# Gates and values by seven products of half the width: a gated MLP's up projection after Strassen, residual stream in DRAM

## The chip, the core and the metric

The kernel runs on one core of a Trainium2 chip. The time is the device time of one execution in microseconds (us). The core has a matrix engine (TensorE, PE in the profile, its weight loads PEld), a vector engine (VectorE, DVE), a scalar engine (ScalarE, ACT), GpSimd (POOL), and SyncE (SP), whose queue issues most of the DMA transfers. PE reads its operands from the on-chip memory SBUF and adds its products into PSUM, which holds eight banks of 128 partitions x 512 floats; ACT and DVE read both memories.

## What is computed

One layer of a diffusion backbone over 512 latent tokens and 256 context tokens of width 2048, in float32: modulation vectors from `c`, two attention mixers (eight heads of differential attention, eight of latent attention), an output projection, and a gated MLP. The change is in the MLP, which is this, with `h` of 512 x 2048, `w_up` of 2048 x 11264, `w_down` of 5632 x 2048:

```
h2 = modulate(rmsnorm(x, norm2_w), sh2, s2)
g, u = split(h2 @ w_up)                               # 512 x 5632 each
g = conv over tokens of width 3 (centred) + bias
x = x + g2 * ((silu(g) * u) @ w_down)
return rmsnorm(x, final_w)
```

## The kernel before

Everything lies feature-first: a tile has 128 features on the partitions and the tokens along the row, so an activation tile is 128 x 512. A matrix product in float32 is made of three passes over operands in a faster 32-bit format: each operand is split into a high part (a rounding cast on ACT, line 75) and a low part (the difference, on DVE, line 76), and `mm3` (lines 96 to 101) adds high x high, high x low and low x high into the same PSUM tile, one `matmul` each.

Weights come from DRAM in blocks of 128 x 1024 (512 KB) through `wblock` (lines 82 to 89): a DMA on SP's queue into `wr`, then the split into `wh` and `wl`; each of the three has three buffers. Eight weight tiles of 128 x 128 are in one block.

PSUM: two `s` tiles of 1024 columns (two banks each, `s_tile`) and four `b` tiles of one bank (`b_tile`).

The stages are: the modulation vectors and first projection (to about 180 us), the input projection (to about 470), the two attentions (to about 880), the output projection (to about 1050), the second norm, and the MLP (from about 1062 to 2511), then the final norm and the stores.

The MLP has 44 pairs. A pair `ft` is 128 features of the gate and the 128 features of the value that multiply them. `up(ft)` (lines 736 to 745) makes both, the gate into the left half of an `s` tile and the value into the right half: for each, 16 row blocks of K (2048 / 128) times three matmuls of 128 x 512. `first_pair` makes the first two pairs together, row block by row block, in both `s` tiles, since their operands `hx` come from the norm just then. `activate` (lines 747 to 760) is the convolution (ACT, then two fused multiplies on DVE), SiLU on ACT, the product on DVE and the split into `ah` and `al`. After four pairs (a chunk; `FC` is 4, and there are eleven) `down` (lines 762 to 774) multiplies the four activations by their part of `w_down`: 16 output tiles, each four row blocks of three matmuls into a `b` tile, and a fused multiply and add on DVE (line 771) into `x1`, the residual stream, which stays in SBUF in the 16 tiles of the pool `bp`. The chunks overlap: the four pairs of chunk c are issued before `down` of chunk c - 1. The last `down` runs in two halves of 256 tokens, so that the final norm of the first half lies beside the second.

Pools are reused tile by tile: an instruction that writes a buffer waits for the last reader of the tile that was there. The language's scheduler puts the instructions of each engine in a fixed order when the program is built, by the order of the code and its own estimate of when each can start, and inserts the semaphore waits. On the chip each engine goes through its list in that order.

Of the kernel before, what the change touches and what calls it, by code (L numbers as in the profile page):

```python
# [17 lines left out]
P = 128  # L18
D = 2048
KT = D // P  # L20
T = 512
# [13 lines left out]
FC = 4  # L35
NFC = NFT // FC
# [13 lines left out]
def layer_kernel(ctx: ExitStack, tc: tile.TileContext, small, rope, c_row, cc_row, x_t, ctx_t, ada, ada_k,  # L50
                 w_g0, w_f, w_v, w_uqn, w_uqr, w_ukv, w_o, w_up0, w_up, w_dn, out_t):
    nc = tc.nc
# [49 lines left out]


    sm = ctx.enter_context(tc.tile_pool(name="sm", bufs=1))
    sm.tile([P, 96], F32, name="edge")
    rim = ctx.enter_context(tc.tile_pool(name="rim", bufs=1, side="right"))
    rim.tile([P, 120], F32, name="rim")


    smt = cst.tile([P, NSMALL], F32, name="smt")  # L110
# [3 lines left out]
        o = OFF[name] + j  # L114
        return smt[:, o:o + 1]

    ropet = cst.tile([P, 2, T], F32, name="ropet")
# [52 lines left out]
    def a2k(dt=F32):  # L170
        return ap_.tile([P, 512], dt, tag="a2k", name=nm("a2k"))
# [246 lines left out]
    q = rtmp()  # L418
# [176 lines left out]
    mb = None  # L595
    nxt = latent_pair(0)
    da.release()
    bp = ctx.enter_context(tc.tile_pool(name="bp", bufs=16, reuse_waits="tile"))

    def b2k(dt=F32):  # L600
        return bp.tile([P, 512], dt, tag="b2k", name=nm("b2k"))
# [38 lines left out]
    mb.release()  # L640
    ma.release()
    mc.release()
    ps_b.release()
    ps_b = ctx.enter_context(tc.tile_pool(name="ps_c", bufs=4, space=PSUM, reuse_waits="tile"))


    ap_ = tc.alloc_tile_pool(name="ap2", bufs=32, side="right", reuse_waits="tile")
    wo = tc.alloc_tile_pool(name="wo", bufs=1, reuse_waits="tile")
    cb = wo.tile([P, D], F32, name="cb2")
# [16 lines left out]
    def token_norm(pool, ss, last):  # L666

        n = ss.shape[1]
        po = b_tile()[:, :n]
        pe.matmul(po, ones32, ss, start=True, stop=False)  # L670
        for i, x in enumerate(last):
            q = pool.tile([P, T], F32, tag="sq", name=nm("sq"), bufs=2)[:, :n]
            sc.square(q, x)
            pe.matmul(po, ones32, q, start=False, stop=i == len(last) - 1)
        r, t1, t2 = (pool.tile([P, T], F32, tag=g, name=nm(g), bufs=1)[:, :n] for g in ("nr", "n1", "n2"))
        rstd(r, po, D, t1, t2)
        return r

# [29 lines left out]
    r = token_norm(wo, ss, x1[12:])  # L708
    hx = []
    for dt in range(KT):  # L710
        t = wo.tile([P, T], F32, tag="xr", name=nm("xn"), bufs=3)
        ve.tensor_tensor(t, x1[dt], r, op=ALU.mult)
        h = wo.tile([P, T], F32, tag="h", name=nm("h"), bufs=2)
        sc.activation(h, t, AF.Identity, scale=a2[:, dt:dt + 1], bias=modx[:, 48 + dt:49 + dt])
        hl = a2k(F32R), a2k(F32R)
        split(hl[0], hl[1], h)
        hx.append(hl)
    wo.release()


    ff = tc.alloc_tile_pool(name="ff", bufs=1, reuse_waits="tile")

    def first_pair():

        ss_ = [s_tile(), s_tile()]
        for kb in range(8):
            wh, wl = wblock(w_up0[kb])
            for j in range(2):
                kt = kb * 2 + j
                for i in range(4):  # L730
                    o = j * 512 + i * P
                    mm3(ss_[i // 2][:, (i % 2) * 512:(i % 2 + 1) * 512], (wh[:, o:o + P], wl[:, o:o + P]), hx[kt],
                        kt == 0, kt == KT - 1)
        return [activate(ft, s) for ft, s in enumerate(ss_)]

    def up(ft):
        s = s_tile()
        for i in range(2):
            o = s[:, i * 512:(i + 1) * 512]
            for hf in range(2):  # L740
                wh, wl = wblock(w_up[ft - 2, i, hf])
                for j in range(8):
                    kt = hf * 8 + j
                    mm3(o, (wh[:, j * P:(j + 1) * P], wl[:, j * P:(j + 1) * P]), hx[kt], kt == 0, kt == KT - 1)
        return activate(ft, s)

    def activate(ft, s):
        g, u = s[:, :512], s[:, 512:]
        t = ff.tile([P, T], F32, tag="t", name=nm("t"), bufs=2)
        sc.activation(t, g, AF.Identity, scale=col("cw", NFT + ft), bias=col("cb", ft))  # L750
# [5 lines left out]
        a = ff.tile([P, T], F32, tag="sq", name=nm("a"), bufs=2)  # L756
        ve.tensor_tensor(a, t, u, op=ALU.mult)
        hl = [ff.tile([P, T], F32R, tag=g_, name=nm(g_), bufs=6) for g_ in ("ah", "al")]
        split(hl[0], hl[1], a)
        return hl  # L760

    def down(c, acts, ts=slice(0, T), then=None):
        for dp in range(8):
            wh, wl = wblock(w_dn[c, dp])
            for i in range(2):
                dt = dp * 2 + i
                po = b_tile()[:, :ts.stop - ts.start]
                for f in range(FC):
                    o = f * 256 + i * P
                    mm3(po, (wh[:, o:o + P], wl[:, o:o + P]), [a[:, ts] for a in acts[f]], f == 0, f == FC - 1)  # L770
                ve.scalar_tensor_tensor(out=x1[dt][:, ts], in0=po, scalar=modx[:, 80 + dt:81 + dt],  # L771
                                        in1=x1[dt][:, ts], op0=ALU.mult, op1=ALU.add)
                if then:
                    then(dt)

    acts = first_pair() + [up(ft) for ft in range(2, FC)]
    for c in range(1, NFC):
        nxt = [up(c * FC + f) for f in range(FC)]
        down(c - 1, acts)
        acts = nxt  # L780


    norms = []
    for th in range(2):
        ts = slice(th * 256, (th + 1) * 256)
        ss = ff.tile([P, 256], F32, tag="ss", name=nm("ss"), bufs=2)
        down(NFC - 1, acts, ts, lambda dt: add_square(ff, ss, x1[dt][:, ts], dt == 0) if dt < 12 else None)
        norms.append(ss)
    exp_ln_tables()
    for th in range(2):  # L790
        ts = slice(th * 256, (th + 1) * 256)
        r = token_norm(ff, norms[th], [x[:, ts] for x in x1[12:]])
        for dt in range(KT):
            y = a2k()[:, :256]
            ve.scalar_tensor_tensor(out=y, in0=x1[dt][:, ts], scalar=col("fw", dt), in1=r, op0=ALU.mult, op1=ALU.mult)
            nc.sync.dma_start(out_t[dt][:, ts], y)
    ff.release()
    ap_.release()


# [77 lines left out]
```

## Time and profile before

| | us |
|---|---|
| median of 3 runs (lowest to highest) | 2538.99 (2534.21 to 2539.63) |
| the profiled execution | 2537.23 |
| its span, first to last instruction | 2535.5 |
| PE busy | 2457.9 |
| DVE busy | 1368.1 |
| ACT busy | 820.6 |
| POOL busy | 97.7 |
| DMA, HBM read and written | 331.68 MB and 23.34 MB, 140 GB/s |

The profile is one execution. Its page gives the busy time of each engine, the same in 40 slices with the clock granted to PE (PEclk, 1.00 is full) and the DMA share, the chain of waits that ended last, and groups of instructions by line: busy time, mean duration in ns, idle time of the engine just before them and what released it. The views asked of the trace beside it are the timeline (start, duration, engine, line, tiles), the same groups by shape, and the sums over stretches of time (windows). A name such as `wh` stands for all buffers of that name. Matmuls are pipelined: a duration runs from the start to the landing of the result and overlaps the next ones, so the distance of starts is what one costs.

### The profile page before, as it was taken

Reading aid. Unit: us, or ns where it says so; the run is one execution under the profiler, and the core shown is the slowest. Engines: PE = TensorE matmul, PEld = TensorE weight load, DVE = VectorE, ACT = ScalarE, POOL = GpSimd, SP = SyncE. Lnnn points to the kernel's source line nnn. Section 1 sums busy time; section 2 is a strip of 40 time slices with the busy share of each in tenths; the row PEclk is TensorE's granted clock in tenths of the full one; section 3 lists DMA queues with packets and bytes.
Section 4 is the critical chain, followed back from the end, with each engine's and each line's share of the span. In section 5 each row is a group of like instructions: output and inputs, shape, how many; then the busy total and the mean of one; then the engine's idle time right before and its main releaser. Section 6 shows DMA issues by size and latency. Waiting matters only on the chain.

```text
span 2535.5 us, 29404 instructions
## 1 busy us (share of the span) xinstructions
PE 2457.9 (97%) x11852; PEld 2003.8 (79%) x11852; DVE 1368.1 (54%) x1779; ACT 820.6 (32%) x1189; POOL 97.7 (4%) x90
## 2 busy tenths in 40 slices
PE   7999999999899999899999999999999999999996
PEld 3778887777777788778888888888888888888886
DVE  4778876498787875533444434343434343434356
ACT  4342221265555622432222222222222222222223
POOL 0000000221100012000000000000000000000003
PEclk9999999999999999999999999999999999999998
DMA  7868898544211185223323223323323333233234
GB/s 276 286 220 320 325 333 307 173 136 135 89 58 55 49 314 197 84 85 99 100 92 100 100 92 100 99 93 100 98 93 100 95 96 100 94 98 100 93 102 146
DMA packets 105214, 356.94 MB, mean 141 GB/s; under 512 B 11379, under 2 KB 22131, under 8 KB 96627
## 3 DMA queue, kind: packets, MB, share of 16 engines
q1 hardware_dynamic: 104118, 351.92, 41.7%
q0 software_dynamic: 960, 3.15, 0.3%
q8 instruction: 93, 1.52, 0.2%
q14 instruction: 43, 0.35, 0.0%
HBM read 331.68 MB, written 23.34 MB: 140 GB/s over the span
## 4 chain that ended last, share of the span: by engine, by line
PE 90%; DVE 6%; ACT 2%; POOL 1%; issue 1%; DMA 1%; DVEq 0%; ACTq 0%; POOLq 0%
PE s L99 16%; PE s L100 16%; PE s L101 16%; PE b L100 10%; PE b L99 10%; PE b L101 10%; PE s L475 3%; PE f L99 1%; PE pt L487 1%; PE f L100 1%; DVE m L477 1%; PE f L101 1%; DVE p L533 1%; PE b L212 1%; PE po L99 1%; POOL p L532 1%
## 5 line engine op out<-in xcount | busy, mean ns | idle before, releaser
L76 DVE TENSOR_TENSOR wl<-wr,wh 128x1024 fp32r<-128x1024 f32 (+2 forms) x382 | 458.8, 1201 | 724.8 <-ACT wh L75 712.9
L75 ACT CAST wh<-wr 128x1024 fp32r<-128x1024 f32 (+2 forms) x382 | 394.3, 1032 | 1142.2 <-PE s L100 668.7
L99 PE MATMUL s<-a2k,wh 128*128 128x512 f32 x1600 | 625.9, 392 | 15.2 <-ACT a2k L75 6.4
L100 PE MATMUL s<-a2k,wh 128*128 128x512 f32 x1600 | 625.9, 391 | 0.0
L101 PE MATMUL s<-a2k,wl 128*128 128x512 f32 x1600 | 625.6, 391 | 0.0
L99 PEld LDWEIGHTS s<-a2k,wh 128*128 128x128 f32 x1600 | 301.4, 189 | 79.2 <-ACT a2k L75 7.6
L100 PEld LDWEIGHTS s<-a2k,wh 128*128 128x128 f32 x1600 | 301.6, 189 | 62.2 <-issue 1.2
L101 PEld LDWEIGHTS s<-a2k,wl 128*128 128x128 f32 x1600 | 301.5, 188 | 62.3 <-issue 0.6
L100 PE MATMUL b<-al,wh 128*128 128x512 f32 (+1 forms) x768 | 285.2, 371 | 0.0
L101 PE MATMUL b<-ah,wl 128*128 128x512 f32 (+1 forms) x768 | 285.2, 371 | 0.0
L99 PE MATMUL b<-ah,wh 128*128 128x512 f32 (+1 forms) x768 | 285.2, 371 | 0.0
L771 DVE SCALAR_TENSOR_TENSOR b2k<-b,modx,b2k 128x512 f32<-128x512 f32 (+1 forms) x192 | 135.1, 705 | 169.0 <-PE b L101 168.7
L164 DVE CUSTOM_DVE_ANT_0 ada<-ada,cb,smt 128x2048 f32<-128x2048 f32 x64 | 151.4, 2368 | 45.6 <-DMA ada<-in_ada 45.4
L100 PEld LDWEIGHTS b<-al,wh 128*128 128x128 f32 x768 | 144.7, 188 | 25.0
L101 PEld LDWEIGHTS b<-ah,wl 128*128 128x128 f32 x768 | 144.7, 188 | 24.9
L99 PEld LDWEIGHTS b<-ah,wh 128*128 128x128 f32 x768 | 144.7, 188 | 24.9
L99 PE MATMUL b<-a2k,wh 128*128 128x512 f32 x304 | 119.7, 394 | 1.6 <-ACT wh L75 1.6
L100 PE MATMUL b<-a2k,wh 128*128 128x512 f32 x304 | 119.5, 393 | 0.0
L101 PE MATMUL b<-a2k,wl 128*128 128x512 f32 x304 | 118.5, 390 | 0.0
L664 POOL TENSOR_TENSOR ss<-ss,sq 128x256 f32<-128x256 f32 (+1 forms) x33 | 45.2, 1371 | 1764.0 <-ACT sq L663 1762.9
L477 DVE TENSOR_REDUCE m<-s 128x1 f32<-128x768 f32 x96 | 90.5, 950 | 15.6 <-PE s L475 15.3
L76 DVE TENSOR_TENSOR wtl<-pt,wth 128x512 fp32r<-128x512 f32 x92 | 63.2, 687 | 20.8 <-ACT wth L75 20.1
(250 smaller groups left out, 2963.7 us busy)
## 6 DMA issues: line engine op xcount, KB each, us to landing
wr<-in_w_up SPq DMA_DIRECT2D x176, 512.0 KB, 3.4
ada<-in_ada SPq DMA_DIRECT2D x64, 1024.0 KB, 6.0
wr<-in_w_dn SPq DMA_DIRECT2D x96, 512.0 KB, 3.4
wr<-in_w_f SPq DMA_DIRECT2D x34, 512.0 KB, 6.4
adak<-in_ada_k SPq DMA_DIRECT2D x32, 512.0 KB, 6.7
ada<-in_ada SPq DMA_DIRECT2D x32, 512.0 KB, 6.8
wr<-in_w_o SPq DMA_DIRECT2D x32, 512.0 KB, 3.5
wr<-in_w_v SPq DMA_DIRECT2D x16, 512.0 KB, 6.8
```

The costliest lines, as they stand in the source:

```text
L75: sc.copy(dst_h, src)
L76: ve.tensor_tensor(dst_l, src, dst_h.bitcast(F32), op=ALU.subtract)
L99: pe.matmul(out, st[0], mv[0], start=start, stop=False, **kw)
L100: pe.matmul(out, st[0], mv[1], start=False, stop=False, **kw)
L101: pe.matmul(out, st[1], mv[0], start=False, stop=stop, **kw)
L164: ve.tensor_tensor_reduce(out=junk, in0=w, in1=vec, op0=ALU.mult, op1=ALU.add, scale=1.0, scalar=col("b_ada", j), accum_out=dst[:, j:j + 1])
L212: pe.matmul(acc[32 * c:32 * c + 32, :n], cpad[:, kt], src(kt), start=j == 0, stop=j == 3)
L475: pe.matmul(s[:, c0:c1], a, b[:, c0:c1], start=i == 0, stop=i == len(mms) - 1)
L477: ve.tensor_reduce(out=m, in_=s[:, :TT], axis=AX.X, op=ALU.max, negate=True)
L487: pe.transpose(pt[:, qt * P:(qt + 1) * P], ws[qt][:, kt * P:(kt + 1) * P], ident)
L664: gp.tensor_tensor(out=ss, in0=ss, in1=q, op=ALU.add)
L771: ve.scalar_tensor_tensor(out=x1[dt][:, ts], in0=po, scalar=modx[:, 80 + dt:81 + dt], in1=x1[dt][:, ts], op0=ALU.mult, op1=ALU.add)
```

## The change

For pairs 4 to 43 the products for gate and value are regrouped. K is cut in two halves (row blocks 0 to 7 and 8 to 15), the tokens in two halves of 256, and the two outputs of a pair (gate and value) are the third cut. That is a 2 x 2 by 2 x 2 block product, and Strassen's scheme (in Winograd's form) makes it with seven block products in place of eight, each of 8 row blocks x 128 columns x 256 tokens, and additions of operands and results:

- The operand sums `t1` to `t4` over halves of h (with low parts, like all operands) are made once, after the second norm (`sums`), and kept in SBUF; `h11` (first half of K, first half of the tokens) and `h2` (second half of K, all tokens) are kept too. `h12` is needed for the first four pairs only.
- The weight sums are made for every pair on DVE (four sums of 128 x 1024 in `strassen`), and each of the seven weight blocks is then split into high and low.
- Results gather in `y` and `z` (256 columns in each half of an `s` tile) and `x` (a `b` tile); `m1`, `m5` and `u2` are copied to SBUF by ACT on the way, and DVE adds them to the others.

Pairs 0 to 3 are made the former way; as the first half of K now lies in two tiles by tokens, its matmuls there are 256 wide (`classical`). `first_pair` uses the four `b` tiles, and takes the row blocks in another order (0, 4, 1, 5, ...). The norm's shift and scale go into one fused multiply and the split itself.

The residual stream goes to DRAM: `x1_d` is written after the output projection (DMA on POOL's queue), `down` loads each tile before it adds to it (DMA on SP's queue, three buffers `xs`), and stores it again (POOL's queue). The last `down` loads into 16 tiles and keeps them there. The order of the chunks is now: first pair of chunk c, `down` of chunk c - 1, the other three pairs. `ah` and `al` have five buffers (six before).

The diff, cut to its core:

```diff
+    x1_d = [dram.tile([P, T], F32, name=f"x1_d{i}") for i in range(KT)]
...
             x1.append(x)
+            gp.dma_start(x1_d[dt], x)
...
+    def normed(kt):
+        b = modx[:, 48 + kt:49 + kt]
+        h = hf[kt] = hp.tile([P, T], F32, tag="h", name=nm("h"), bufs=5)
+        ve.scalar_tensor_tensor(out=h, in0=x1[kt], scalar=a2[:, kt:kt + 1], in1=r, op0=ALU.mult, op1=ALU.mult)
...
+        for (hh, hl), c in parts:
+            sc.activation(hh, h[:, c], AF.Identity, bias=b)
+            ve.scalar_tensor_tensor(out=hl, in0=h[:, c], scalar=b, in1=hh.bitcast(F32), op0=ALU.add, op1=ALU.subtract)
...
+    def sums(j):
+        a, c, b = hf[j], hf[j + 8], modx[:, 56 + j:57 + j]
...
+        ve.tensor_tensor(d1, a[:, h1], a[:, h0], op=ALU.subtract)
+        ve.scalar_tensor_tensor(out=d2, in0=c[:, h1], scalar=b, in1=d1, op0=ALU.add, op1=ALU.subtract)
+        put_away(t1, d1)
+        ve.scalar_tensor_tensor(out=d1, in0=c[:, h1], scalar=db[:, j:j + 1], in1=a[:, h1], op0=ALU.add, op1=ALU.subtract)
+        put_away(t3, d1)
+        ve.scalar_tensor_tensor(out=d1, in0=c[:, h0], scalar=b, in1=d2, op0=ALU.add, op1=ALU.subtract)
+        put_away(t2, d2)
+        put_away(t4, d1)
+
+    def classical(out, kt, w, start, stop):
+        if kt < 8:
+            mm3(out[:, h0], w, h11[kt], start, False, True)
+            mm3(out[:, h1], w, h12[kt], False, False, True)
+        else:
+            mm3(out, w, h2[kt], False, stop, True)
...
+    def strassen(ft):
+        s = s_tile()
+        y, z, x = s[:, :HT], s[:, 512:512 + HT], b_tile()[:, :HT]
...
+        def product(out, w, hs, start, stop=True):
+            wh, wl = (wp.tile([P, 1024], F32R, tag=g, name=nm(g), bufs=3) for g in ("wh", "wl"))
+            split(wh, wl, w)
+            for j in range(8):
+                mm3(out, (wh[:, j * P:(j + 1) * P], wl[:, j * P:(j + 1) * P]), hs[j], start and j == 0, j == 7, True)
+
+        def kept(src, tag):
+            t = mm.tile([P, HT], F32, tag=tag, name=nm(tag), bufs=1)
+            sc.copy(t, src)
+            return t
+
+        a11, a21, a22, a12 = raw(0, 0, wp), raw(1, 0, wp), raw(1, 1, mm), raw(0, 1, mm)
...
+        product(y, a11, h11, True)                                  # P1
+        m1 = kept(y, "m1")
+        w = mm.tile([P, 1024], F32, tag="ws", name=nm("ws"), bufs=1)
+        ve.tensor_tensor(w, a21, a22, op=ALU.add)
+        product(z, w, t1, True)                                     # P2
+        m5 = kept(z, "m5")
+        ve.tensor_tensor(w, w, a11, op=ALU.subtract)
+        product(y, w, t2, False)                                    # P3
+        u2 = kept(y, "u2")
+        product(x, a12, h21, True)                                  # P4
+        ve.tensor_tensor(g[:, h0], x, m1, op=ALU.add)
+        ve.tensor_tensor(a11, a11, a21, op=ALU.subtract)
+        product(y, a11, t3, False)                                  # P5
+        ve.tensor_tensor(m5, y, m5, op=ALU.add)
+        ve.tensor_tensor(w, a12, w, op=ALU.subtract)
+        product(z, w, h22, False)                                   # P6
+        ve.tensor_tensor(g[:, h1], z, u2, op=ALU.add)
+        product(y, a22, t4, False)                                  # P7
+        return activate(ft, g, (y, m5))
...
+                x = dst[dt] if dst else mm.tile([P, T], F32, tag="xs", name=nm("xs"), bufs=3)
+                if ts.start == 0:
+                    nc.sync.dma_start(x, x1_d[dt])
...
-                ve.scalar_tensor_tensor(out=x1[dt][:, ts], in0=po, scalar=modx[:, 80 + dt:81 + dt],
-                                        in1=x1[dt][:, ts], op0=ALU.mult, op1=ALU.add)
+                ve.scalar_tensor_tensor(out=x[:, ts], in0=po, scalar=modx[:, 80 + dt:81 + dt],
+                                        in1=x[:, ts], op0=ALU.mult, op1=ALU.add)
                 if then:
                     then(dt)
+                else:
+                    gp.dma_start(x1_d[dt], x)
...
     for c in range(1, NFC):
-        nxt = [up(c * FC + f) for f in range(FC)]
+        nxt = [strassen(c * FC)]
         down(c - 1, acts)
-        acts = nxt
+        acts = nxt + [strassen(c * FC + f) for f in range(1, FC)]
```

The marks P1 to P7 are added here; they name the seven products in the prediction.

More of the change, by code (lines that the diff above doesn't have):

```diff
@@ L597, in layer_kernel @@
     da.release()
-    bp = ctx.enter_context(tc.tile_pool(name="bp", bufs=16, reuse_waits="tile"))
+    bp = tc.alloc_tile_pool(name="bp", bufs=16, reuse_waits="tile")
     def b2k(dt=F32):
@@ L707, in layer_kernel @@
                                 in1=col("n2", dt), op0=ALU.add, op1=ALU.mult)
[L708 to L717, printed above, removed]
+    db = sm.tile([P, 8], F32, name="db")
@@ L718, in layer_kernel, with half @@
+    ve.tensor_tensor(db, modx[:, 56:64], modx[:, 48:56], op=ALU.subtract)
     wo.release()
     ff = tc.alloc_tile_pool(name="ff", bufs=1, reuse_waits="tile")
+    hp = tc.alloc_tile_pool(name="hp", bufs=1, side="right", reuse_waits="tile")
+    h0, h1 = slice(0, HT), slice(HT, T)
+    r = token_norm(hp, ss, x1[12:])
+    def half(t):
+        return t[:, h0], t[:, h1]
+    hf, h11, h12, h2, t1, t2, t3, t4 = ([None] * KT for _ in range(8))
+    def normed(kt):
[3 more added lines that the diff above has]
+        if kt < 8:
+            h11[kt] = half(a2k(F32R))
+            h12[kt] = half(hp.tile([P, T], F32R, tag="h12", name=nm("h12"), bufs=8))
+            parts = ((h11[kt], h0), (h12[kt], h1))
+        else:
+            h2[kt] = a2k(F32R), a2k(F32R)
+            parts = ((h2[kt], slice(0, T)),)
+        for (hh, hl), c in parts:
+            sc.activation(hh, h[:, c], AF.Identity, bias=b)
+            ve.scalar_tensor_tensor(out=hl, in0=h[:, c], scalar=b, in1=hh.bitcast(F32), op0=ALU.add, op1=ALU.subtract)
@@ new lines, in layer_kernel, with put_away @@
+    spare = [tp.tile([P, T], F32R, tag="tp", name=nm("tp")) for _ in range(8)]
+    def sums(j):
+        a, c, b = hf[j], hf[j + 8], modx[:, 56 + j:57 + j]
+        d1, d2 = (hp.tile([P, HT], F32, tag="d", name=nm("d"), bufs=2) for _ in range(2))
+        def put_away(t, src):
+            t[j] = half(a2k(F32R) if t is t1 else spare.pop(0) if spare else b2k(F32R))
+            split(t[j][0], t[j][1], src)
+        ve.tensor_tensor(d1, a[:, h1], a[:, h0], op=ALU.subtract)
[6 more added lines that the diff above has]
+        put_away(t4, d1)
@@ L723, in first_pair @@
+    def classical(out, kt, w, start, stop):
+        if kt < 8:
+            mm3(out[:, h0], w, h11[kt], start, False, True)
+            mm3(out[:, h1], w, h12[kt], False, False, True)
+        else:
+            mm3(out, w, h2[kt], False, stop, True)
     def first_pair():
-        ss_ = [s_tile(), s_tile()]
-        for kb in range(8):
+        outs = [b_tile() for _ in range(4)]
+        order = [kb for j in range(4) for kb in (j, j + 4)]
+        for n_, kb in enumerate(order):
             wh, wl = wblock(w_up0[kb])
@@ L729, in first_pair @@
                 kt = kb * 2 + j
+                normed(kt)
+                if n_ and n_ % 2 == 0:
+                    sums(n_ - 2 + j)
                 for i in range(4):
                     o = j * 512 + i * P
-                    mm3(ss_[i // 2][:, (i % 2) * 512:(i % 2 + 1) * 512], (wh[:, o:o + P], wl[:, o:o + P]), hx[kt],
-                        kt == 0, kt == KT - 1)
-        return [activate(ft, s) for ft, s in enumerate(ss_)]
+                    classical(outs[i], kt, (wh[:, o:o + P], wl[:, o:o + P]), kt == 0, kt == KT - 1)
+        return [activate(ft, outs[2 * ft], half(outs[2 * ft + 1])) for ft in range(2)]
     def up(ft):
@@ L755, in activate, with down @@
         sc.activation(t, t, AF.Silu)
-        a = ff.tile([P, T], F32, tag="sq", name=nm("a"), bufs=2)
-        ve.tensor_tensor(a, t, u, op=ALU.mult)
-        hl = [ff.tile([P, T], F32R, tag=g_, name=nm(g_), bufs=6) for g_ in ("ah", "al")]
+        a = ff.tile([P, T], F32, tag="t", name=nm("a"), bufs=2)
+        for c, u_ in zip((h0, h1), u):
+            ve.tensor_tensor(a[:, c], t[:, c], u_, op=ALU.mult)
+        hl = [ff.tile([P, T], F32R, tag=g_, name=nm(g_), bufs=5) for g_ in ("ah", "al")]
         split(hl[0], hl[1], a)
         return hl
-    def down(c, acts, ts=slice(0, T), then=None):
+    def down(c, acts, ts=slice(0, T), dst=None, then=None):
         for dp in range(8):
```

58 lines of the change are left out of this document (40 added, 18 removed).

## The prediction

> **What bounds the kernel now.** I read the page first: busy shares, slices, the chain that ended last, the costliest groups.
>
> ```profile
> span 2535.5 us, 29404 instructions
> PE 2457.9 (97%) x11852; PEld 2003.8 (79%) x11852; DVE 1368.1 (54%) x1779; ACT 820.6 (32%) x1189; POOL 97.7 (4%) x90
> PE 90%; DVE 6%; ACT 2%; POOL 1%; issue 1%; DMA 1%; DVEq 0%; ACTq 0%; POOLq 0%
> L99 PE MATMUL s<-a2k,wh 128*128 128x512 f32 x1600 | 625.9, 392 | 15.2 <-ACT a2k L75 6.4
> ```
>
> TensorE is the bound, and the 128x512 matmuls behind lines 99 to 101 carry it. Then the stretches: the MLP's steady part, and three others that the clock needs below.
>
> ```profile
> core 0: us, PE busy (x) PEld busy (x) DVE busy (x) ACT busy (x) POOL busy (x), PEclk, DMA share, GB/s
> 700.00:880.00 180.00, 171.90 (x931) 136.66 (x930) 143.76 (x252) 102.47 (x198) 0.00 (x0) 1.00 0.14 44
> 670.00:690.00 20.00, 16.97 (x86) 13.38 (x85) 13.51 (x23) 9.09 (x19) 1.97 (x2) 0.83 0.07 24
> 1114.00:1118.00 4.00, 4.00 (x11) 3.02 (x11) 0.70 (x2) 0.06 (x1) 0.00 (x0) 0.50 0.00 0
> 1416.00:1634.00 218.00, 218.00 (x963) 180.53 (x962) 82.93 (x88) 55.95 (x62) 0.00 (x0) 1.00 0.30 97
> ```
>
> In 1416:1634 PE never stops, at full clock, and DVE is 38% busy: this stage ends on matmul count times spacing. Busy times overlap (392 ns each), so the price of a matmul is the distance of starts, from the timeline of PE:
>
> ```profile
> 2379.75 0.39 PE L100 MATMUL s<-a2k,wh 128*128 128x512 f32 x1
> ...
> 2390.18 0.39 PE L101 MATMUL s<-a2k,wl 128*128 128x512 f32 x1
> ...
> 2479.76 0.28 PE L100 MATMUL b<-al,wh 128*128 128x256 f32 x1
> ...
> 2483.00 0.28 PE L100 MATMUL b<-al,wh 128*128 128x256 f32 x1
> ```
>
> The first two are 46 starts apart: 0.2267 us per 512 columns. The last two, in the final half-width down projection, are 27 apart: 0.1200 us per 256, more than half (0.1134). The result comes 0.283 us after a start.
>
> **The change, part by part. Matmuls.** A pair before: 4 blocks x 8 x 3 = 96 x 0.2267 = 21.77 us. After: 7 products x 8 x 3 = 168 x 0.1200 = 20.16. So 1.60 less per pair, 64 us over 40 pairs, if PE never waits. [...]
>
> **The waits that come with it.** Seven products share two PSUM accumulators of one tile (y and z), and a third x; three of them (m1, m5, u2) are copied out on ACT, and every accumulation into y or z waits for the read before it. In the program as built, that holds across the whole tile: z's next product waits for a copy of y too. PE's fixed order over one pair in steady state (P1 to P7 as in the code; P1' is the next pair's):
>
> ```
> P1 18 | P4 2 | P2 24 | P4 11 | P3 24 | P4 11 | P5 24 | P1' 1 | P6 24 | P1' 5 | P7 24
> ```
>
> With three weight buffers, P4's weights go where P1's were, P5's where P2's, P6's where P3's, P1' where P5's. So each cast (line 75) starts only when the product three back has ended, and in ACT's queue it stands ahead of the copy that PE waits for. Prices:
>
> ```profile
> L76 DVE TENSOR_TENSOR wl<-wr,wh 128x1024 fp32r<-128x1024 f32 x358 | 439.7, 1228 | 720.3 <-ACT wh L75 708.6 <-PE s L101 3.3
> L76 DVE TENSOR_TENSOR mvl<-f,mvh 128x256 fp32r<-128x256 f32 x24 | 10.0, 422 | 4.2 <-ACT mvh L75 3.9
> L771 DVE SCALAR_TENSOR_TENSOR b2k<-b,modx,b2k 128x512 f32<-128x512 f32 x160 | 120.1, 750 | 162.7 <-PE b L101 162.6
> L75 ACT CAST wh<-wr 128x1024 fp32r<-128x1024 f32 x358 | 377.3, 1054 | 1135.6 <-PE s L100 668.7 <-PE b L100 344.8 <-PE b L101 82.6
> L214 ACT COPY row<-b 128x256 f32<-128x256 f32 x8 | 3.0, 371 | 13.4 <-PE b L212 13.4
> ```
>
> ```profile
> 836.02 0.59 ACT L75 CAST wth<-pt 128x512 fp32r<-128x512 f32 x1
> ...
> 836.66 0.50 PE L99 MATMUL po<-wth,mvh 128*128 128x512 f32 x1 [0.73 <-ACT wth L75]
> ...
> 2398.79 0.39 PE L100 MATMUL s<-a2k,wh 128*128 128x512 f32 x1
> 2399.22 1.06 ACT L75 CAST wh<-wr 128x1024 fp32r<-128x1024 f32 x1 [4.38 <-PE s L100]
> 2400.17 0.78 ACT L750 ACTIVATE t<-s,smt 128x512 f32<-128x512 f32 x1
> ...
> 2509.04 0.28 PE L101 MATMUL b<-ah,wl 128*128 128x256 f32 x1
> ...
> 2509.36 0.48 DVE L771 SCALAR_TENSOR_TENSOR b2k<-b,modx,b2k 128x256 f32<-128x256 f32 x1 [0.96 <-PE b L101]
> ```
>
> From these: a reader starts 0.04 us after a matmul's result; ACT starts its next instruction 0.95 after a 1024-wide cast's start; PE starts 0.05 after ACT ends, and its first matmul then takes 0.11 longer (0.50 for 0.39). Counting from the moment a product's slots end:
>
> - A, after P1: cast of P4's weights 0.08 to 1.14; P4's two matmuls 1.19 to 1.54; the m1 copy ends at 1.40, so P2 starts at 1.54. Lost: 1.54 - 0.24 = 1.30.
> - B, after P2, and C, after P3: cast to 1.14, copy 1.03 to 1.40, PE at 1.56 with its late first matmul; eleven P4 matmuls cover 1.32. Lost 0.24 each.
> - D, after P5: cast of P1' to 1.14, its one matmul to 1.42, P6 behind it. Lost 1.42 - 0.12 = 1.30. The DVE sum that P6 also needs (0.20 + 0.42) is ready sooner.
> - E, after P6: DVE sum to 0.62, PE at 0.78, five matmuls cover 0.60. Lost 0.18.
>
> That is 3.26 us lost for 1.60 gained: a pair takes 23.42 us instead of 21.77. In ten pairs, the first of each group of four, down-projection matmuls stand where P1' would: D is only the sum, 0.78, and E 0.10; 2.66 lost. Together 30 x 3.26 + 10 x 2.66 = 124 us. Bounds: latencies 0.15 smaller or larger at A and D and 0.1 at B and C make 104 to 145.
>
> DVE does seven lows and four sums of 128x1024 a pair, spaced 1.15 (1228 ns less overlap), 12.7, and 3.8 of small work (three half-width sums near 0.35, the two convolution steps 0.72, two halves of the product 0.34, one low 0.62): 16.5 of 23.4, hidden. ACT has 9.8 (seven casts, three copies, 2 of activation), hidden but for the order above. Weights load a product or more ahead.
>
> **First two pairs and the norm.** Splitting the first half of K by tokens turns 64 groups (4 x 8 in the first two pairs, 2 x 2 x 8 in the next two) of 3 x 0.2267 into 6 x 0.1200: +2.6. Before, the third pair waited for the first two's PSUM, and PE came back at half clock:
>
> ```profile
> 1107.97 0.39 PE L101 MATMUL s<-a2k,wl 128*128 128x512 f32 x1
> 1112.68 0.79 PE L99 MATMUL s<-a2k,wh 128*128 128x512 f32 x1 [4.32 <-DVE a L757]
> ...
> 1118.34 0.40 PE L100 MATMUL s<-a2k,wh 128*128 128x512 f32 x1
> ```
>
> From 1107.97 to 1118.34 lie 14 starts, worth 3.2 us; 7.2 are lost. The first two pairs now sit in four other PSUM tiles, so I take all of it back: -7.2 (bounds 0 to -7.2). Ahead of them the norm's first operand takes one pass less:
>
> ```profile
> 1059.40 3.10 DVE L712 TENSOR_TENSOR xn<-b2k,nr 128x512 f32<-128x512 f32 x5
> ...
> 1062.21 1.22 PE L99 MATMUL s<-a2k,wh 128*128 128x512 f32 x2 [6.41 <-ACT a2k L75]
> ...
> L325 ACT ACTIVATE c2k<-h,modc 128x256 fp32r<-128x256 f32 x16 | 8.1, 504 | 0.0
> ```
>
> From the first xn to the first matmul 2.81 us; now a fused multiply (0.75 as line 771's), a half-width bias on ACT (0.50) and 0.05: -1.5. The four operand sums add DVE work: 16 fused multiplies at 0.68, 8 wide lows at 0.70, 16 half ones at 0.42, some 50 half-width sums and lows at 0.38, 6 weight lows at 1.15, 49 us beside 44.8 of matmuls. DVE falls behind PE only for the last four row blocks, by 2 to 4 us, and there the third pair's matmuls stand between in PE's order: +1 (0 to +6).
>
> **Residual in DRAM.** Per down projection 16 loads on SP and 16 stores on POOL of 256 KB, three buffers. One buffer's round must fit three output tiles of 12 x 0.2267 = 8.16 us.
>
> ```profile
> L463 POOL DMA_DIRECT2D v_d<-kh x6: 752/752/945, 472.0 to 486.8; - x6
> DMA to landing us min/median/max: 2.7/6.0/12.2
> wr<-in_w_up SPq DMA_DIRECT2D x176, 512.0 KB, 3.4
> xr<-in_x_t SPq DMA_DIRECT2D x16, 256.0 KB, 3.9
> v_d<-kl POOLq DMA_DIRECT2D x6, 256.0 KB, 7.3
> ```
>
> Eviction 0.75, store 2.7 (quiet) to 7.3 (its row, in a burst), load 2.7 to 3.9, 0.3 of handing over: 6.5 to 12.3. The MLP's DMA share is 0.30, so I stand near the quiet end, 7.3, and within. Behind a late load wait, on SP, two down blocks and the next pair's weights, and on DVE, behind its eviction, the lows. Both run two blocks (10.9 us) ahead. I take +2; at 12.3 a projection would end (12.3 - 8.16) x 13 / 3 = 18 late, less about 11 of slack: +7 each, +70. The 16 stores in the output projection (16 x 0.75 on POOL) hide under its matmuls, and the last stage's 16 loads start as the last pair frees its operands, some 15 us early: nothing (bound +5).
>
> **Sum.** -64.3 + 124.4 + 2.6 - 7.2 - 1.5 + 1 + 2 = +57, on the profiled execution's 2537.2 (span 2535.5 and 1.7 around it): 2594. The median of the runs shown, 2539.0, is 1.8 above; forecast 2596, +2.2%. What tells apart from no change here is about 0.2%, 5 us.
>
> **Rivals.**
> - PE stays fed (faster). If casts and copies end within their covers, a pair takes 20.16 and the sum is 57 - 124 = -67: 2472. It decides at a loss per pair of (64.3 + 3.1) / 40 = 1.68 us; I count 3.11. For it: ACT is a third busy and copies are short. Against it: each copy stands behind a 1.05 us cast that cannot start earlier. With it go cases of half the loss, 62 us: about 2534.
> - The residual's round is too long: 30 to 70 more, 2626 to 2666. For it: 7.3 in the burst; against it: share 0.30.
> - The clock drops at the gaps. The 4.32 us gap cost half of it (0.50 in 1114:1118). Three shorter ones within 4 us are followed by 0.83 (670:690), a single one of 1.35 leaves 1.00 (700:880):
>
> ```profile
> 674.97 0.50 PE L475 MATMUL s<-knh,qnh 128*128 128x512 f32 x1 [0.74 <-ACT p L479]
> 676.60 0.50 PE L100 MATMUL po<-wtl,v 128*128 128x512 f32 x1 [0.66 <-DVE wtl L76]
> 678.69 0.48 PE L487 MATMUL pt<-ident,p 128*128 128x128 f32 x1 [1.03 <-DVE p L533]
> ...
> 708.19 0.50 PE L475 MATMUL s<-knh,qnh 128*128 128x512 f32 x1 [1.35 <-ACT w L479]
> ```
>
> A and D lie 8 us apart, which speaks against. At 2.7 us lost (12 starts at twice their distance) once a pair: +108, 2704. [...]
>
> **How the numbers follow.** Forecast, 2565 to 2620: 0.72. Residual's round: 0.11. Clock: 0.05. PE fed or half fed: 0.12, of it 0.02 within 0.2%. Slower 0.88, same 0.02, faster 0.10. The range leaves out the clock, the fed PE and the top of the residual's case: 2558 to 2650.
>
> **What would show it.** PE idle in the pairs rises from nothing to about 3 us a pair, put down to ACT at lines 75 and 821 (wh, m, u), in two gaps near 1.3. A stretch of four pairs and a projection, 130.6 before, takes about 137 (3 x 23.42 + 22.82 + 43.5). The 4.32 gap is gone. Gaps under 0.3 at A or D would prove me wrong, as would idle time of evictions on loads beyond a few us a projection, or PEclk under 0.95 in the pairs.

## The result and the profile after

The changed kernel takes 2600.8 us (median; 2595.4 to 2606.8) against 2539.3; the ratio, taken over the runs of both, is 1.0246, 95% interval 1.0217 to 1.0274. The profiled execution has a span of 2593.6 us, 58.1 more than before.

The page of the changed kernel: the share of PE, the chain that ended last, and two of the costliest groups (busy, mean ns of one, then the engine's idle time before them and what ended it).

```profile
span 2593.6 us, 37486 instructions
...
PE 2440.8 (94%) x14924; PEld 2108.2 (81%) x14924; DVE 1746.5 (67%) x2296; ACT 974.0 (38%) x1453; POOL 192.3 (7%) x266
...
PE 72%; DVE 11%; ACT 7%; DMA 5%; issue 3%; POOL 1%; SPq 0%; ACTq 0%; DVEq 0%; POOLq 0%
...
L99 PE MATMUL s<-a2k,wh 128*128 128x256 f32 (+1 forms) x1216 | 369.5, 308 | 39.8 <-ACT wh L75 29.6
...
L99 PE MATMUL b<-a2k,wh 128*128 128x256 f32 (+1 forms) x688 | 235.3, 344 | 47.5 <-ACT wh L75 42.4
```

Before, 90% of the chain was PE. Now 72% is, and DVE, ACT and DMA hold 23% where they held 9%: by line, the casts of line 75 hold 5% of it, their lows 3%, and the residual's loads and stores 2% each. The two matmul groups name the releaser, line 75 on ACT, although ACT is busy for only 38% of the span.

All that PE waited for between 1200 and 2520 us, by releaser (us in total, times, longest):

```profile
engine line waited for: us in total, times, longest us
PE b L99 <- ACT wh L75: 40.9, 39, 1.6
PE s L99 <- ACT wh L75: 29.6, 29, 1.0
PE s L99 <- DVE m L840: 5.2, 10, 0.5
PE b L101 <- DVE wl L76: 2.5, 5, 0.7
PE s L99 <- ACT u L821: 0.3, 1, 0.3
```

The same question between 1300 and 2400 us of the kernel before has no row at all. Here the first row is the fourth product's first matmul (tile b is x), once a pair: gap A (39 times; pair 4 lies ahead of the stretch). The second is the next pair's first matmul ahead of P6, in the 29 pairs that have one (I had counted 30): gap D. The third is D in pairs where none stands there. Gaps B, C and E are not listed; they can be read from the starts. Idle time is counted from the landing of the last result, 0.28 us after its start, so these rows show less than the starts lose: 78.5 us here. PE's timeline over one steady pair (start, duration, then in brackets the idle time and its releaser):

```profile
1543.02 0.28 PE L101 MATMUL s<-a2k,wl 128*128 128x256 f32 x1
1544.31 0.38 PE L99 MATMUL b<-a2k,wh 128*128 128x256 f32 x1 [1.02 <-ACT wh L75]
1544.54 0.28 PE L100 MATMUL b<-a2k,wh 128*128 128x256 f32 x1
...
1548.76 0.28 PE L99 MATMUL b<-a2k,wh 128*128 128x256 f32 x1
1549.01 0.39 PE L99 MATMUL s<-tp,wh 128*128 128x256 f32 x1
...
1553.18 0.28 PE L101 MATMUL b<-a2k,wl 128*128 128x256 f32 x1
1553.48 0.38 PE L99 MATMUL s<-tp,wh 128*128 128x256 f32 x1
...
1557.63 0.50 PE L99 MATMUL s<-a2k,wh 128*128 128x256 f32 x2 [1.02 <-ACT wh L75]
...
1561.21 0.28 PE L101 MATMUL s<-a2k,wl 128*128 128x256 f32 x1
1561.41 0.39 PE L99 MATMUL s<-tp,wh 128*128 128x256 f32 x1
...
1567.73 0.38 PE L99 MATMUL b<-a2k,wh 128*128 128x256 f32 x1 [1.02 <-ACT wh L75]
```

From one fourth product to the next, 1544.31 to 1567.73, lie 23.42 us. Where PE waits for nothing, starts are 0.12 apart (1541.82 to 1543.02: ten of them). At A the distance is 1.29 and the next one 0.23 instead of 0.12; at B it is 0.25, at C 0.30, at D 1.29, at E 0.20. After every such wait the second matmul comes 0.10 late as well.

ACT's own timeline in the same stretch shows why:

```profile
1543.22 1.04 ACT L75 CAST wh<-wr 128x1024 fp32r<-128x1024 f32 x1
1544.17 0.36 ACT L821 COPY m<-s 128x256 f32<-128x256 f32 x1
...
1556.54 1.04 ACT L75 CAST wh<-wr 128x1024 fp32r<-128x1024 f32 x1 [2.06 <-PE s L100]
```

The last matmul of P1 started at 1543.02; the cast that reuses its weight buffer starts at 1543.22, and the copy of m1, which needs no more than P1's end either, stands behind it until 1544.17. PE's next matmul after P1 is one of P4's, which needs that cast; it starts at 1544.31, 0.05 after the cast's end. The third row is the same at gap D: the cast for P1' starts at 1556.54, 0.20 after P5's last matmul (1556.34), and PE goes on at 1557.63.

A group of four pairs and a projection, and the nine groups from the first to the tenth projection together (us, busy time of each engine, granted clock, DMA share, GB/s):

```profile
core 0: us, PE busy (x) PEld busy (x) DVE busy (x) ACT busy (x) POOL busy (x), PEclk, DMA share, GB/s
1309.42:1446.14 136.72, 128.93 (x867) 117.71 (x866) 87.76 (x100) 48.11 (x60) 8.64 (x16) 1.00 0.46 154
1172.71:2406.30 1233.59, 1160.18 (x7778) 1059.24 (x7777) 790.47 (x900) 432.72 (x540) 77.83 (x144) 1.00 0.46 154
```

A group takes 136.7 us at best and 1233.59 / 9 = 137.07 on average, against 130.56 before. The granted clock is 1.00 in both stretches.

### The profile page after: what moved, and what is told of

Read it like the earlier page. It is cut to its first block, busy times and chain, and to the rows that moved or that the text cites. A ratio compares the mean times of both kernels' runs of the same rounds, so it can differ in the third digit from the quotient of the medians.

```text
span 2593.6 us, 37486 instructions
## 1 busy us (share of the span) xinstructions
PE 2440.8 (94%) x14924; PEld 2108.2 (81%) x14924; DVE 1746.5 (67%) x2296; ACT 974.0 (38%) x1453; POOL 192.3 (7%) x266
## 4 chain that ended last, share of the span: by engine, by line
PE 72%; DVE 11%; ACT 7%; DMA 5%; issue 3%; POOL 1%; SPq 0%; ACTq 0%; DVEq 0%; POOLq 0%
PE s L99 12%; PE s L100 10%; PE s L101 10%; PE b L99 10%; PE b L100 9%; PE b L101 9%; ACT wh L75 5%; DVE wl L76 3%; PE s L477 2%; DMA xs<-x_d 2%; DMA x_d<-xs 2%; DVE ws L833 1%; PE f L99 1%; PE pt L489 1%; DVE m L479 1%
## 5 line engine op out<-in xcount | busy, mean ns | idle before, releaser
L99 PE MATMUL s<-a2k,wh 128*128 128x256 f32 (+1 forms) x1216 | 369.5, 308 | 39.8 <-ACT wh L75 29.6
L100 PE MATMUL s<-a2k,wh 128*128 128x256 f32 (+1 forms) x1216 | 368.1, 304 | 0.0
L101 PE MATMUL s<-a2k,wl 128*128 128x256 f32 (+1 forms) x1216 | 367.8, 303 | 0.0
L99 PE MATMUL b<-a2k,wh 128*128 128x256 f32 (+1 forms) x688 | 235.3, 344 | 47.5 <-ACT wh L75 42.4
L75 ACT CAST wh<-ws 128x1024 fp32r<-128x1024 f32 x120 | 125.9, 1049 | 399.3 <-DVE ws L833 129.4
L99 PEld LDWEIGHTS s<-a2k,wh 128*128 128x128 f32 x1216 | 229.2, 191 | 57.4 <-ACT wh L75 35.4
L76 DVE TENSOR_TENSOR wl<-ws,wh 128x1024 fp32r<-128x1024 f32 x120 | 146.7, 1223 | 148.4 <-ACT wh L75 144.8
L100 PEld LDWEIGHTS s<-a2k,wh 128*128 128x128 f32 x1216 | 231.9, 191 | 8.5 <-issue 1.4
L101 PE MATMUL b<-a2k,wl 128*128 128x256 f32 (+1 forms) x688 | 231.7, 337 | 2.5 <-DVE wl L76 2.5
L100 PE MATMUL b<-a2k,wh 128*128 128x256 f32 (+1 forms) x688 | 232.2, 337 | 0.2 <-DVE a2k L747 0.2
L875 DVE SCALAR_TENSOR_TENSOR xs<-b,modx,xs 128x512 f32<-128x512 f32 x160 | 119.8, 749 | 157.8 <-DMA xs<-x_d 98.5
L99 PEld LDWEIGHTS b<-a2k,wh 128*128 128x128 f32 x688 | 130.8, 191 | 65.6 <-ACT wh L75 50.7
L99 PE MATMUL s<-b2k,wh 128*128 128x256 f32 x640 | 181.1, 283 | 0.0
L100 PE MATMUL s<-b2k,wh 128*128 128x256 f32 x640 | 181.1, 283 | 0.0
```

Of the source, the lines that this page charges most:

```text
L75: sc.copy(dst_h, src)
L76: ve.tensor_tensor(dst_l, src, dst_h.bitcast(F32), op=ALU.subtract)
L99: pe.matmul(out, st[0], mv[0], start=start, stop=False, **kw)
L100: pe.matmul(out, st[0], mv[1], start=False, stop=False, **kw)
L101: pe.matmul(out, st[1], mv[0], start=False, stop=stop, **kw)
L875: ve.scalar_tensor_tensor(out=x[:, ts], in0=po, scalar=modx[:, 80 + dt:81 + dt], in1=x[:, ts], op0=ALU.mult, op1=ALU.add)
```

## The experiments

Each ran beside the kernel before on the same chip (there at 2536.7 to 2538.8 us); a ratio is to that kernel. Profiles are compared over groups, or from the MLP's first matmul to the end of the span: that matmul stands at 1060.6 to 1066.4 us in the twelve profiles of the changed kernel and its variants, although they do the same work before it. The question was which of the two parts of the loss is the cause: the casts that wait for a weight buffer, or the reads of y and z that PE waits for because the two share a tile. The first run removes the sharing, the second the worst of the late casts.

**y and z in tiles of their own (e1).**

```
+    ps_b.release()
+    ps_s.release()
+    ps_y = ctx.enter_context(tc.tile_pool(name="ps_y", bufs=4, space=PSUM, ...))
+    ps_b = ctx.enter_context(tc.tile_pool(name="ps_d", bufs=4, space=PSUM, ...))
...
-        s = s_tile()
-        y, z, x = s[:, :HT], s[:, 512:512 + HT], b_tile()[:, :HT]
+        y, z = (ps_y.tile([P, 512], F32, tag="s", ..., bufs=4)[:, :HT] for _ in range(2))
+        x = b_tile()[:, :HT]
```

> The accumulators y and z get a PSUM tile (one bank) each instead of sharing one; the three weight buffers stay, so each cast still waits for the product three back. In the program as built PE's order becomes P1 to P7, 24 matmuls each, with nothing drawn ahead. Theory (casts that start late AND copies behind them that PE waits for, because a read of y holds up z): with a whole product of 2.88 us of the other accumulator between a copy and the next use, cast (1.05) and copy (0.37) fit, a pair takes 20.16 to 20.4 us, the kernel 2596 - 124 = about 2472 (2468 to 2485). Rival 1 (the three weight buffers alone are the cause): casts start as late as before, a pair stays at 22.5 to 23.4, 2565 to 2600. Rival 2 (DVE, 16.5 us of work a pair, becomes the bound once PE is faster): a pair of 21 to 22, 2505 to 2545.

2476.4 us, ratio 0.9763 (0.9748 to 0.9777). The four PSUM banks of the two large tiles are the same four, now handed out one at a time. PE's order changed with them, as the expectation says. The worst group, then one without gaps:

```profile
1301.75:1428.93 127.18, 124.66 (x867) 116.79 (x866) 87.68 (x101) 48.01 (x60) 8.65 (x16) 1.00 0.51 166
1803.34:1927.52 124.18, 124.18 (x867) 116.67 (x865) 88.21 (x101) 48.01 (x60) 8.65 (x16) 1.00 0.52 170
```

124.18 us with PE busy in all of it is 4 x 20.16 plus 192 x 0.2267 for the projection (124.17): the pairs run at their matmuls' spacing. The weight buffers are still three and each cast still waits for the product three back (in the profile of e5, the same kernel, casts of line 75 wait for matmuls of line 100 223 times between 1200 and 2400 us, 523.3 us in all), so rival 1 falls; DVE, 88 of 124 us busy, is not the bound, so rival 2 falls too. The worst group is 3 us over; e6 below takes that up.

**The fourth product's weights in buffers of their own (e2)**, y and z still sharing.

```
-            wh, wl = (wp.tile([P, 1024], F32R, tag=g, name=nm(g), bufs=3) for g in ("wh", "wl"))
+            wh, wl = ((mm if own else wp).tile(..., bufs=1 if own else 3) for g in ("wh", "wl"))
...
-        u2 = kept(y, "u2")
-        product(x, a12, h21, True)
+        u2 = kept(y, g[:, h1])
+        product(x, a12, h21, True, own=True)
```

> The fourth product's weights get buffers of their own, so their cast need not wait for the end of P1 (to make room, u2 is copied into the half of g where it ends up); y and z still share a tile. In the program as built the m1 copy now stands ahead of every cast that waits for P1, and P1's first matmuls stand before P7, not P6. Theory: gap A (1.30) goes, D falls to the DVE sum of m5 (0.78 - 0.12 = 0.66), E stays 0.18: a pair of about 21.1, and 2596 - 40 x 2.2 = about 2508 (2490 to 2525). Rival (the reads of the shared tile cost the time, whatever stands ahead of them): A stays near 1, a pair above 22.5, 2560 to 2600.

2545.9 us, ratio 1.0036 (1.0023 to 1.0048): 55 us less than the changed kernel (53 by the ratios), 38 more than I expected. Nine groups, then PE in the first two pairs of one group, and ACT just before:

```profile
1174.63:2361.52 1186.89, 1151.91 (x7778) 1056.73 (x7777) 794.35 (x901) 435.37 (x541) 77.83 (x144) 1.00 0.49 160
```

```profile
1631.45 0.39 PE L99 MATMUL s<-tp,wh 128*128 128x256 f32 x1 [1.10 <-ACT g L821]
...
1635.10 0.39 PE L99 MATMUL s<-a2k,wh 128*128 128x256 f32 x1 [0.52 <-DVE m L840]
...
1644.25 0.28 PE L99 MATMUL b<-a2k,wh 128*128 128x256 f32 x1
1644.52 0.38 PE L99 MATMUL s<-a2k,wh 128*128 128x256 f32 x1
1644.74 0.28 PE L100 MATMUL s<-a2k,wh 128*128 128x256 f32 x1
...
1656.58 0.39 PE L99 MATMUL s<-a2k,wh 128*128 128x256 f32 x1 [0.52 <-DVE m L840]
```

```profile
1630.08 1.04 ACT L75 CAST wh<-wr 128x1024 fp32r<-128x1024 f32 x1 [3.15 <-issue]
1631.03 0.37 ACT L821 COPY g<-s 128x256 f32<-128x256 f32 x1
```

A group takes 1186.89 / 9 = 131.9, where 4 x 21.1 + 43.5 = 127.9 was expected: 4.0 a group, 40 in all, the whole miss. The wait for the cast at A is gone and D is the DVE sum, as forecast; 1635.10 to 1656.58 is 21.48 a pair, 0.4 above my figure, because P2 and P3 still wait for the copies of m1 and m5: P2's first matmul, at 1644.52, stands 0.27 behind the last where 0.12 is the spacing, and the next comes 0.10 late. Most of the rest lies in the first pair of a group: there u2 stands behind a cast, and PE waits 1.10. Moving one cast moved the place of the wait; with the tile shared, PE still waits for copies and sums of the tile it is to write.

**The change without Strassen's products (e3).**

```
-        nxt = [strassen(c * FC)]
+        nxt = [up(c * FC)]
...
-        acts = nxt + [strassen(c * FC + f) for f in range(1, FC)]
+        acts = nxt + [up(c * FC + f) for f in range(1, FC)]
```

(The second halves of the first operand move to a pool that lives as long as the loop.)

> All of the change but Strassen's products: the 40 pairs are done by the classical blocks on the new operand layout (operand sums are still formed, residual still in DRAM). A block of the first half of K costs 6 x 0.1200 instead of 3 x 0.2267, 0.04 us more, 16 of them a pair: +25.5. With -7.2 (gap), -1.5 (first operand), +2.6, +1 and +2 from the prediction: 2539 + 22 = about 2561 (2553 to 2570). Rival (the residual's round trip costs 30 to 70): 2590 or more.

2564.5 us, ratio 1.0111 (1.0096 to 1.0126).

```profile
1447.59:1580.87 133.28, 133.28 (x769) 118.15 (x768) 51.88 (x60) 32.67 (x37) 8.65 (x16) 1.00 0.48 158
```

PE is never idle with the residual in DRAM, so that rival falls. A group is 2.72 longer than before, where 4 x 0.64 = 2.55 was the price of the split blocks. The run lies 27.8 above the kernel before that ran beside it, where 22 was forecast; from the MLP's first matmul to the end its profile is 26.1 longer (1499.4 against 1473.2) and 23.9 was forecast. Of these 2.2, 1.7 lie in ten groups; the rest of the difference lies ahead of the MLP and was not followed.

**No residual traffic (e4).**

```
-                if ts.start == 0:
+                if ts.start == 0 and dst:
...
+                else:
+                    ve.tensor_scalar(out=x, in0=po, scalar1=modx[...], scalar2=None, op0=ALU.mult)
...
-                else:
-                    gp.dma_start(x1_d[dt], x)
```

> The changed kernel without the residual's traffic: the ten down projections inside the loop load and store nothing and scale their result into a tile that is dropped (so that part of the residual sum is left out). Priced at +2 in the prediction: about 2 us less than the changed kernel, 2598 (2590 to 2603). Rival (the round trip holds up the projections): 30 us less or more, below 2571.

2595.6 us, ratio 1.0230 (1.0215 to 1.0246): some 5 us below the changed kernel's median, within the range and far from 30. The intervals of the two ratios overlap; from the MLP's first matmul to the end the profiles are 1530.1 us here and 1533.0 in the changed kernel, 2.9 apart.

**The rests of the best version.** The kernel with separate tiles again (e5), then with six residual buffers (e6; the edit shown below at the changed kernel), without the residual's traffic (e7), with the fourth product's own weight buffers (e8), and with the last two together (e9).

> The kernel with y and z in tiles of their own once more, as the base of the next three: 2476 (2473 to 2479).

2479.3 us, ratio 0.9771 (0.9758 to 0.9784).

> As the base, with six residual buffers instead of three. In the base, a group of four pairs and a projection takes 124.18 us in four of ten, and 0.2 to 3.0 more in the others, 5.5 us in all, with DVE evictions that wait up to 4.6 us for a residual load. Theory (those rests are late residual loads, which six buffers ask for earlier): about 5 us less, 2471 (2469 to 2474). Rival (they are weight loads or chance): 2476, no change.

2474.8 us, ratio 0.9751 (0.9737 to 0.9764), 4.5 below its base, with intervals that overlap a little. From the first projection to the last (the same matmuls in both), first this run, then its base:

```profile
1182.37:2404.01 1221.64, 1221.64 (x8474) 1146.61 (x8473) 869.08 (x982) 470.08 (x587) 86.71 (x160) 1.00 0.52 172
```

```profile
1181.26:2404.87 1223.61, 1222.38 (x8474) 1146.77 (x8473) 863.46 (x982) 470.02 (x587) 86.72 (x160) 1.00 0.52 173
```

With six buffers PE is busy in every microsecond of it. In this profile the base lost 2.0 us there, in the first profile of the same kernel (e1) 5.5. The profiles carry this; the times alone do not.

> As the base, without the residual's loads and stores in the ten projections inside the loop (that part of the residual sum is left out). Theory: every group takes 124.2, 2470 (2468 to 2473), the least that the residual's traffic can cost here being 5 us. Rival (the rests come from elsewhere): 2476.

2473.8 us, ratio 0.9747 (0.9734 to 0.9761): what six buffers give, within the intervals. All nine groups of its profile take 124.18. This median, e5's and e6's each lie less than 1 us above their ranges. The rests came from the residual's traffic. That its late loads are what counts is borne out by e6, where more buffers do nothing but let loads start sooner: between 1200 and 2400 us DVE waited for residual loads 59 times in e5, 90.2 us in all, and e6 has no such row.

> As the base, and the fourth product's weights in buffers of their own. Theory (late casts cost nothing by themselves once no read of y holds up z): no change, 2476 (2472 to 2480). Rival (late casts still cost some): 10 us less or more, below 2467.

2497.3 us, ratio 0.9840 (0.9826 to 0.9853): neither no change nor a gain, but 18 us lost. ACT and SP in a group of 127.2 us:

```profile
1612.49 0.36 ACT L821 COPY g<-s 128x256 f32<-128x256 f32 x1
1621.49 1.99 ACT L75 CAST wh<-wr 128x1024 fp32r<-128x1024 f32 x2 [8.64 <-DMA wr<-in_w_up]
```

```profile
1612.36 0.32 SPq L870 DMA_DIRECT2D xs<-x_d  x1
1612.78 5.71 SPq L810 DMA_DIRECT2D wr<-in_w_up  x2
```

A cast of weights that had not been loaded holds ACT for 8.64 us, and the next two casts come behind it, the second of them at 1623.39. Between 1200 and 2400 us PE waits 12 times for a low of line 76, 9.4 us in all. The loads go out behind residual loads in SP's queue (the second row covers two of them, up to 1618.5). Whether those residual loads are what makes them late is the question of the next run, which has the edits of e4 and e8 together.

> The kernel with tiles apart and the fourth product's own weight buffers (2497, 18 more than its base), now without the residual's loads and stores in the ten projections of the loop (that part of the residual sum is left out). Theory (with weight buffers free early, ACT's casts stand in front of weight loads that wait on SP behind residual loads; ACT idles up to 8.8 us on them): without the residual's loads it comes back to the base without them, 2474 (2470 to 2478). Rival (the buffers or the order of the casts cost by themselves): 2488 or more.

2477.8 us, ratio 0.9750 (0.9727 to 0.9773). Every group takes 124.18 again, so the groups' loss went with the residual's traffic: a buffer that is free sooner had only drawn a cast ahead, in ACT's queue, of a load that was late. The rest above 2474 lies ahead of the groups: from the MLP's first matmul to the first projection it is 119.19 us here and 115.59 in e7, and in the fifth pair PE waits 1.86 us for a cast and 2.27 for its low.

**Six residual buffers in the changed kernel alone (e10).**

```
-                x = dst[dt] if dst else mm.tile([P, T], F32, tag="xs", name=nm("xs"), bufs=3)
+                x = dst[dt] if dst else mm.tile([P, T], F32, tag="xs", name=nm("xs"), bufs=6)
```

> The changed kernel with six residual buffers instead of three, nothing else. Theory (its groups took 136.7 us at best and up to 137.7, 3.4 us in all, through late residual loads): about 4 us less, 2597 (2593 to 2600). Rival (the buffers change nothing): 2601.

2597.0 us, ratio 1.0220 (1.0198 to 1.0242), against 1.0246 with three. The nine groups that took 1233.59:

```profile
1177.06:2407.31 1230.25, 1159.86 (x7778) 1058.93 (x7777) 793.00 (x900) 433.09 (x540) 78.08 (x144) 1.00 0.46 154
```

3.3 us less, 136.69 a group, as the theory had it. The intervals of the two ratios overlap, so the profile carries this more than the times do.

**A version that beats both (e11).** Separate tiles, six residual buffers, and the pool of one-bank tiles set up ahead of the MLP's first pair:

```
+    ps_b.release()
+    ps_s.release()
+    ps_y = ...
+    ps_b = ...
     acts = first_pair()
...
-        s = s_tile()
+        s = [ps_y.tile([P, 512], F32, tag="s", ..., bufs=4) for _ in range(2)]
```

> y and z in tiles of their own, six residual buffers, and the PSUM pool of one-bank tiles set up ahead of the MLP's first pair instead of behind its fourth. Theory (with the pool set up behind the fourth pair, the first matmul of the fifth waited 2.68 us for the reads of the fourth's): 2474.8 - 2.7 = 2472 (2469 to 2475), about 0.974 of the kernel before. Rival (the wait moves to the next reader): 2475.

2472.3 us, ratio 0.9731 (0.9712 to 0.9751): 66 us faster than the kernel before. Against e6 the intervals overlap; from the MLP's first matmul to the end the profile is 2.5 us shorter (1405.7 against 1408.2), with 2.7 forecast. The wait it was to remove, in e1's profile, and this version's busy shares:

```profile
1160.22 0.36 PE L99 MATMUL s<-a2k,wh 128*128 128x256 f32 x1 [2.52 <-DVE a L857]
```

```profile
span 2472.1 us, 37485 instructions
...
PE 2398.5 (97%) x14924; PEld 2101.5 (85%) x14924; DVE 1756.3 (71%) x2296; ACT 973.6 (39%) x1453; POOL 191.2 (8%) x266
```

No such wait is left in this version: behind the MLP's first matmul PE's longest is 0.19 us up to its last.

## Why the prediction was right

The forecast was 2596 (2558 to 2650); 2600.8 came. The sum said +57; the spans of the profiled executions are 58.1 apart, the medians 61.5. How close the spans come is in part chance: of the profiles, this one has the MLP's first matmul earliest, at 1060.6 where others have up to 1066.4. From that matmul to the end it is 1533.0 against 1473.2, 59.7 more, where the sum without the norm's -1.5 says 58.5.

- **Matmuls, -64.3.** Shown by taking the waits away: a group with none (e6) is 124.18 against 130.56, 6.38 less, 63.8 over ten groups. The trace's spacing of 0.1200 held: 4 x 20.16 and the projection's 192 x 0.2267 are 124.17.
- **Waits, +124.4.** Measured: 136.72 - 124.18 = 12.54 a group, 125.4 over ten. A steady pair takes 23.42, the figure forecast; A cost 1.17 + 0.11 and D 1.17 + 0.10 where I had 1.30 each, B and C 0.23 and 0.28 with their late second matmul where I had 0.24, E 0.18. One sign was misread ahead: I said PE's idle time would rise to about 3 us a pair, from ACT at lines 75 and 821. By the profile's count it rises to 1.95 ((136.72 - 128.93) / 4), and nearly all of it is put down to line 75: the loss of 3.26 shows in the starts.
- **What causes them.** My account named two things together, the cast that cannot start before its buffer is free and the read that holds both accumulators. e1 and e2 show that they are not equal. Take the shared tile away and the casts cost nothing (124.18 a group); take the worst cast away and the shared tile still costs (131.9, which is 1.9 a pair). e1 changed PE's order as well, so the order drawn up for the shared tile would be a rival. The changed kernel's first Strassen pair (pair 4, the fifth) speaks against it. There P1 and P2 stand in plain order, no cast stands ahead of the copy of m1, and PE waits for that copy all the same:

```profile
1156.46 0.37 ACT L821 COPY m<-s 128x256 f32<-128x256 f32 x1 [2.03 <-PE s L101]
1156.89 0.39 PE L99 MATMUL s<-a2k,wh 128*128 128x256 f32 x1 [0.46 <-ACT m L821]
```

  P2, P3 and P6 come 0.72, 0.49 and 0.84 late in it, second matmuls counted: 2.05, where a steady pair loses 3.26. The tile's sharing is the condition; the late casts at A and D go with the other 1.2.
- **First pairs and norm.** The 4.32 gap is gone, and the first matmul comes 1.35 us after the first fused multiply of the norm, where it was 2.81:

```profile
1059.24 1.41 DVE L737 SCALAR_TENSOR_TENSOR h<-b2k,a,nr 128x512 f32<-128x512 f32 x2
...
1060.59 0.80 PE L99 MATMUL b<-a2k,wh 128*128 128x256 f32 x2 [5.03 <-ACT a2k L746]
...
1094.25 0.50 PE L100 MATMUL b<-a2k,wh 128*128 128x512 f32 x1 [0.18 <-DVE a2k L747]
```

  -1.46 for -1.5. The 0.18 is the longest idle time up to the first Strassen pair, so the operand sums hide. The first matmul of the fifth pair, before and after:

```profile
1158.93 0.39 PE L99 MATMUL s<-a2k,wh 128*128 128x512 f32 x1
```

```profile
1153.40 0.28 PE L99 MATMUL s<-a2k,wh 128*128 128x256 f32 x1
```

  From the MLP's first matmul (1062.21 and 1060.59) that is 96.71 and 92.81: -3.9, where +2.6 - 7.2 + 1 = -3.6 was forecast. The four terms summed to -5.1 and measure -5.4; 58.1 + 63.8 - 125.4 - 3.3 = -6.8 is what the other terms leave for them, so 1.4 stays unplaced.
- **Residual, +2.** About 3.3 in the profile (e10); the medians lie 3.7 (e10) and 5.2 (e4) lower, with intervals of the ratios that overlap. The term was sized a little low, its mechanism right: the landing times are near the quiet end I took,

```profile
xs<-x_d SPq DMA_DIRECT2D x160, 256.0 KB, 3.0
x_d<-xs POOLq DMA_DIRECT2D x160, 256.0 KB, 3.5
```

  so by the medians a round is an estimated 0.75 (eviction, line 875) + 3.5 + 3.0 + 0.3 (an eviction ends at 1455.54, its store is issued at 1455.83) = 7.55 of the 8.16 that fit, with what loads take longer than their median on top; loads and stores together take 2.2 to 6.2. DVE's evictions did wait on loads, 98.5 us in all and 57 times, 9.9 a projection, more than the few that I said would prove me wrong; yet a group lost only 0.4 on average. That test was badly chosen: most of what the evictions waited was not PE's time here.
- **PE stays fed.** Worked out at 2472 from the same spacing, it is what the kernel gives once y and z are apart: 2476.4, and 2472.3 with six residual buffers and the pool set up earlier. As a forecast for the change as built it was rightly small.
- **Clock.** Gaps of 1.02 us twice in 23.4 left PEclk at 1.00, so that rival falls.

## What to carry to other kernels

Two accumulators in one tile are one object to whoever orders the work: in the programs built here a read of one held up the writes to the other, and the order of the matmuls was drawn up around that. Before counting fewer multiplications as a gain, ask for every accumulator that is read midway what stands ahead of the reader in its engine's queue, and which matmuls cover it; here the tiles' layout was worth 125 us, twice the algorithm's 64. Ask of buffers that free a cast sooner whether its load is there sooner too: in e8 it was not, and the cast held ACT for 8.64 us.

## What the runs showed that was not expected

- The own weight buffers of one product, worth -55 us with the shared tile (e2), cost +18 with separate ones (e8), and nothing in the groups once the residual's traffic was gone (e9), with 3.6 left ahead of them. The same edit changed sign with what else stood in ACT's and SP's queues.
- After each of a steady pair's five waits, from 0.08 to 1.17 us, PE's second matmul comes some 0.10 us late too: 1544.31 to 1544.54 is 0.23 for 0.12. That is about 0.5 of the 3.26.
- The MLP's first matmul stood at 1060.59 in the changed kernel's profile and up to 5.8 us later in its variants, though they do the same work before it. That is more than several of the differences asked about here, so a single profile's span does not show them; its groups do.
